# Gate and up tiles in pairs: wide products of both, then narrow ones, then the down product

## The chip, the cores and the metric

The kernel runs on one core of a Trainium2 chip. A core has a matrix engine (TensorE, "PE" in the profile, with its weight loads as "PEld"), VectorE ("DVE"), ScalarE ("ACT"), GpSimd ("POOL") and SyncE ("SP", which here starts nearly all transfers). Each engine works through its own queue in order. Matrix products are written to PSUM, which has eight banks of 128 x 512 float32; the other operands lie in SBUF.

The metric is the device time of one execution in microseconds (us), as a median of several.

## The reference: what is computed

Two decoder layers on x of 256 tokens by 1024 channels, in float32. Each layer is a feed-forward network (FFN), a mixer with three kinds of attention, and a second FFN:

```python
h = h + 0.5 * swiglu(rms_norm(h, ffn1_norm[l]), ffn1_w_gate[l], ffn1_w_up[l], ffn1_w_down[l])
h = h + hybrid_mixer(rms_norm(h, mix_norm[l]), w_in[l], ...)
h = h + 0.5 * swiglu(rms_norm(h, ffn2_norm[l]), ffn2_w_gate[l], ffn2_w_up[l], ffn2_w_down[l])

def swiglu(x, w_gate, w_up, w_down):
    return (jax.nn.silu(x @ w_gate) * (x @ w_up)) @ w_down
```

The gate and up matrices are 1024 x 2816, the down matrix 2816 x 1024. The change touches only the four FFNs.

## The kernel before

**Two-part numbers.** Every float32 operand of a large product is split into a high part (`wh`, `hh`, xhl's first half) and a low part, the rest (`wl`, `hl`, xhl's second half). A product is the sum high x high + high x low + low x high. For the normed input both parts lie side by side in the tile `xhl`, for each of eight k (128 channels each): 256 columns of high, 256 of low.

**Tiles of an FFN.** The hidden width of 2816 is cut into 22 tiles, f = 0 to 21, of 128. For a gate or up tile, `proj` takes one weight unit of 128 x 1024 and one PSUM bank of the kind `gu` (four banks). It issues eight matmuls 512 wide (the high weights with both parts of xhl, k = 0 to 7), and then eight that are 256 wide (the low weights with the high part). The bank then holds the main sum in its first half and the rest in its second. A down product `down(k)` multiplies one hidden tile with its weights: 24 matmuls of 256 columns into four banks of the kind `acc`. In the last FFN the down product has the tokens as its output rows, and takes 12 matmuls of 512.

**The loop.** For each f, `ffn` (line 356) emits: the gate tile; `gated`, which sums the bank's halves (ACT copies one half, L424; DVE adds the other, L425), multiplies by the norm's factor `norm.rb` (L430) and takes a tanh (L432); for f >= 4, the down product of hidden tile f - 4; `silu` (L450, L451); the up tile; and `hidden`, which sums the up bank (L424, L425), multiplies (L437) and splits the result into `hh` (L441) and `hl` (L444). The order in which these are emitted is the order on each engine's queue; it is written by hand (a manual schedule). A PSUM bank goes to the next tile of its kind when the last reader of the tile that had it is done; banks of one kind are handed out in the order in which they were released.

**Weights.** `Weights` keeps the list of weight units in the order of their use. A raw tile of 1 MB holds two units and is loaded by SP (line 90); five raw tiles can be in flight. `pump` splits one more unit: ACT writes the high part (`high`, L116), DVE the low part one unit later (`low`, L120). `pump` stops when seven units are split and not used; `take` hands out the next unit. The order of the list within an FFN is g(f), d(f - 4), u(f).

**Start and end of an FFN.** The norm's input arrives as `xhl`, k by k, from the tail of the stage before (`tail`, L317 on ACT for the high part, L320 on DVE for the low one), so that the last k, 6 and 7, come when the next FFN has begun. In FFN 1, 2 and 3 the first gate tile is therefore done in two groups of k, 0 to 5 and 6 to 7. The norm's factor comes out of two small products on PE: `norm.sums` (L340), then a power on DVE and POOL (L303, L304), then `norm.broadcast` (L347) and ACT's copy to `rb` (L349). They are placed inside the second and the third tile. Only with `rb` can `gated` finish, so four tiles (g0, u0, g1, u1) are done ahead, in the four `gu` banks. FFN 0 has a start of its own: g0 comes from the program's beginning, and a fifth tile, g2, goes to an `acc` bank. In FFN 3, `turn_trunk` (L383) transposes the residual on PE between u1 and g2. At the end, `tail` (or `finish` in FFN 3) does the last four down products, of f = 18 to 21, bank by bank.

## Time and profile before

| | us |
|---|---|
| median of 3 runs (lowest, highest) | 1060.74 (1060.62, 1060.92) |
| the profiled execution | 1060.79 |
| its span, from the first to the last instruction | 1059.0 |
| PE busy | 1049.5 (99%) |
| DVE busy | 829.4 (78%) |
| ACT busy | 594.9 (56%) |
| POOL busy | 163.7 (15%) |

Matmuls are pipelined: the duration of one in the profile is longer than its distance from the next. What a stream of matmuls costs is therefore read from the starts, not from the durations or the busy share. In rows of the timeline the first two numbers are start and duration in us; "x8" says that eight neighbours were merged; a bracket at the end tells how long the engine stood idle before and what released it. The mean granted clock of PE was 0.998 of full speed.

### The profile page before, as it was taken

The page shows a single profiled execution, that of the slowest core. Times are in us where ns is not written, and L with a number is a line of the kernel's source. Part 1 is how long each engine was busy: PE and PEld are TensorE (multiplying, and loading weights), DVE is VectorE, ACT ScalarE, POOL GpSimd, SP SyncE. Part 2 cuts the span into 40 slices and gives each one's busy share as a digit, 9 for nine tenths or more (in the row PEclk, how much of TensorE's full clock was granted, in tenths as well). Part 3 has the DMA queues.
Part 4 walks back from the last instruction along what each step waited for, and adds up shares of the span by engine and source line. Part 5 has one row for each costly group of instructions (what it writes and reads, how often), then busy time and mean ns, then how long its engine had stood idle before and what let it go on. Part 6 is the DMA issues. An engine that isn't in the chain of part 4 may idle for free.

```text
span 1059.0 us, 16914 instructions
## 1 busy us (share of the span) xinstructions
PE 1049.5 (99%) x6611; PEld 950.0 (90%) x6611; DVE 829.4 (78%) x1560; ACT 594.9 (56%) x1026; POOL 163.7 (15%) x184
## 2 busy tenths in 40 slices
PE   9999999999999999999999999999999999999998
PEld 8999999998799899999999999999978998888887
DVE  6998777779776897777789877777798779877774
ACT  6665554667654665555456555546766555645551
POOL 2004000267700100000010300003766000000000
PEclk9999999999999999999999999999999999999999
DMA  9576464465351365554645565555455214564531
GB/s 327 204 240 200 165 224 152 135 218 171 128 159 41 119 234 173 191 195 163 199 159 197 184 224 167 191 172 179 160 164 184 91 41 156 204 235 161 200 119 40
DMA packets 130912, 181.81 MB, mean 172 GB/s; under 512 B 7008, under 2 KB 104720, under 8 KB 130832
## 3 DMA queue, kind: packets, MB, share of 16 engines
q1 hardware_dynamic: 130512, 180.65, 50.7%
q8 instruction: 52, 0.85, 0.3%
q14 instruction: 28, 0.23, 0.1%
q10 hardware_dynamic: 320, 0.08, 0.0%
HBM read 179.67 MB, written 1.05 MB: 171 GB/s over the span
## 4 chain that ended last, share of the span: by engine, by line
PE 90%; DVE 5%; ACT 3%; issue 1%; DMA 1%; SPq 0%; ACTq 0%; DVEq 0%
PE ps_gu L293 59%; PE ps_acc L293 29%; DVE wl L120 2%; DVE score L728 1%; PE ps_gu L927 1%; DVE xhl L320 1%; DMA xin<-in_x_dram 1%; PE ps_gu L1027 0%; ACT wh L116 0%; ACT tmp L589 0%; DVE hres L352 0%; PE ps_gu L960 0%; ACT L710 0%; ACT L708 0%; DVE tmp L913 0%
## 5 line engine op out<-in xcount | busy, mean ns | idle before, releaser
L120 DVE TENSOR_TENSOR wl<-raw,wh 128x1024 fp32r<-128x1024 f32 (+2 forms) x343 | 416.8, 1221 | 21.8 <-ACT wh L116 21.5
L293 PE MATMUL ps_gu<-xhl,wh 128*128 128x512 f32 (+1 forms) x1408 | 352.6, 392 | 0.9 <-DVE xhl L320 0.7
L116 ACT CAST wh<-raw 128x1024 fp32r<-128x1024 f32 (+2 forms) x343 | 345.2, 1036 | 7.6 <-PE ps_gu L293 3.3
L293 PEld LDWEIGHTS ps_gu<-xhl,wh 128*128 128x128 f32 x1408 | 253.6, 189 | 47.6 <-DVE xhl L320 1.6
L293 PEld LDWEIGHTS ps_gu<-xhl,wl 128*128 128x128 f32 x1400 | 191.8, 190 | 13.7
L293 PE MATMUL ps_gu<-xhl,wl 128*128 128x256 f32 x1400 | 197.2, 283 | 0.0
L293 PE MATMUL ps_gu<-wh,xhl 128*128 128x512 f32 (+2 forms) x512 | 159.4, 381 | 0.0
L425 DVE TENSOR_TENSOR tmp<-ps_gu,tmp 128x256 f32<-128x256 f32 x175 | 74.1, 423 | 105.6 <-ACT tmp L424 105.5
L293 PE MATMUL ps_acc<-hl,wh 128*128 128x256 f32 x528 | 149.7, 284 | 0.0
L293 PE MATMUL ps_acc<-hh,wh 128*128 128x256 f32 x528 | 149.4, 283 | 0.0
L293 PE MATMUL ps_acc<-hh,wl 128*128 128x256 f32 x528 | 149.4, 283 | 0.0
L424 ACT COPY tmp<-ps_gu 128x256 f32<-128x256 f32 x175 | 64.7, 370 | 131.4 <-PE ps_gu L293 125.8
L293 PEld LDWEIGHTS ps_gu<-wh,xhl 128*128 128x128 f32 x512 | 95.7, 190 | 14.7
L293 PEld LDWEIGHTS ps_acc<-hl,wh 128*128 128x128 f32 x528 | 101.3, 192 | 0.3
L293 PEld LDWEIGHTS ps_acc<-hh,wl 128*128 128x128 f32 x528 | 101.4, 192 | 0.0
L293 PEld LDWEIGHTS ps_acc<-hh,wh 128*128 128x128 f32 x528 | 101.3, 192 | 0.0
L293 PE MATMUL ps_gu<-wl,xhl 128*128 128x512 f32 (+2 forms) x256 | 96.4, 377 | 0.0
L331 POOL TENSOR_TENSOR ssacc<-ssacc,tmp 128x512 f32<-128x512 f32 x10 | 13.0, 1297 | 512.5 <-ACT tmp L329 334.3
L432 ACT ACTIVATE tmp<-tmp 128x256 f32<-128x256 f32 x88 | 36.8, 418 | 85.1 <-DVE tmp L430 85.1
L441 ACT CAST hh<-tmp 128x256 fp32r<-128x256 f32 x80 | 32.6, 407 | 86.8 <-DVE tmp L437 86.8
L293 PEld LDWEIGHTS ps_gu<-wl,xhl 128*128 128x128 f32 x256 | 48.5, 190 | 6.8
L451 DVE TENSOR_TENSOR tmp<-tmp,rb 128x256 f32<-128x256 f32 x88 | 37.7, 429 | 3.0
(247 smaller groups left out, 1231.6 us busy)
## 6 DMA issues: line engine op xcount, KB each, us to landing
raw<-in_ffn_w_down_dram SPq DMA_DIRECT2D x44, 1024.0 KB, 6.7
raw<-in_ffn_w_gate_dram SPq DMA_DIRECT2D x43, 1024.0 KB, 7.2
raw<-in_ffn_w_up_dram SPq DMA_DIRECT2D x43, 1024.0 KB, 5.2
raw<-in_w_in_dram SPq DMA_DIRECT2D x24, 1024.0 KB, 5.1
raw<-in_w_out_dram SPq DMA_DIRECT2D x8, 1024.0 KB, 4.8
raw<-in_w_in_dram SPq DMA_DIRECT2D x4, 768.0 KB, 5.2
raw<-in_w_in_dram SPq DMA_DIRECT2D x4, 656.0 KB, 4.3
xin<-in_x_dram SPq DMA_DIRECT2D x4, 256.0 KB, 5.1
```

The lines of the kernel that those rows point to most:

```text
L116: self.nc.scalar.copy(hv, src)
L120: (engine or self.nc.vector).tensor_tensor(lv, self.srcs[self.n_low], hv.bitcast(F32), op=ALU.subtract)
L293: T.matmul(o, l, r, start=start, stop=stop, skip_group_check=True)
L320: V.scalar_tensor_tensor(self.l[:, m], hres[:, m] if src is None else src, gT[:, self.col + m:self.col + m + 1], self.h[:, m].bitcast(F32) ...
L331: G.tensor_tensor(self.acc, self.acc, sq, op=ALU.add)
L424: A.copy(o, ps[:, 1])
L425: V.tensor_tensor(o, ps[:, 0], o, op=ALU.add)
L432: A.activation(th, t_, AF.Tanh, scale=0.5)
L441: (V.tensor_copy if late else A.copy)(hh, t_)
L451: V.tensor_tensor(t_, t_, norm.rb, op=ALU.mult)
L728: V.scalar_tensor_tensor(sc, rl[:, i * n:(i + 1) * n], st["iw"][:, t, h:h + 1], st["cmask"][t] if first else sc, op0=ALU.mult, op1=ALU.add)
L927: T.transpose(b[:, j * P:(j + 1) * P], pj[i][:, j * P:(j + 1) * P], ident)
```

## The change

The list of weight units has u(f) before d(f - 4) now, and a new function `pair` takes two units and two banks at once. It issues all wide matmuls of both tiles, then all narrow ones of both; with groups of k, it does that group by group. The loop calls it for every f whose gate tile was not done early, so that the down product of f - 4 follows both tiles. At the start of FFN 1, 2 and 3, g0 and u0 are one pair in two groups of k; `norm.sums` follows behind it, and `norm.broadcast` stands between the wide and the narrow half of the second pair. In FFN 0 the start stays, and the tile u2 is now emitted ahead of `gated` for f = 2.

```diff
         for f in range(NF):
             half("g", f)
+            half("u", f)
             if f >= DOWN_LAG:
                 half("d", f - DOWN_LAG)
-            half("u", f)
...
+        def pair(groups=(range(KT),), between=None):
+
+            ws = [W.take() for _ in range(2)]
+            pss = [bank("gu").rearrange("p (a b) -> p a b", a=2) for _ in range(2)]
+            for ks in groups:
+                for w, ps in zip(ws, pss):
+                    for k in ks:
+                        mm(ps, w[0][:, k], norm.x[:, k], k == 0, False)
+                if between:
+                    between()
+                for w, ps in zip(ws, pss):
+                    for k in ks:
+                        mm(ps[:, 0], w[1][:, k], norm.h[:, k], False, k == KT - 1)
+            return pss
...
-            g0 = proj(groups=(range(6), range(6, KT)))
+            g0, u0 = pair((range(6), range(6, KT)))
+            norm.sums()
+            W.pump(3)
+            g1, u1 = pair(between=norm.broadcast)
             W.pump()
-            u0 = proj(norm.sums, 5)
-            W.pump(2)
-            g1 = proj(norm.broadcast, 7)
-            W.pump()
-            u1 = proj()
...
         for f in range(1, NF):
-            t_, th = gated(early[f] if f in early else proj())
+            g, u = (early[f], u1 if f == 1 else proj()) if f in early else pair()
+            t_, th = gated(g)
             if f >= DOWN_LAG:
                 down(f - DOWN_LAG)
                 W.pump()
             silu(t_, th)
-            hidden(f, t_, th, u1 if f == 1 else proj())
+            hidden(f, t_, th, u)
```

## The prediction

> **What bounds the kernel now.** I read the page first (one core, span, busy shares), then the chain of waits, then the timeline of TensorE (PE) inside one feed-forward layer (FFN), and last, around each start and end of an FFN, the rows of VectorE (DVE) beside those of PE.

> ```profile
> span 1059.0 us, 16914 instructions
> PE 1049.5 (99%) x6611; PEld 950.0 (90%) x6611; DVE 829.4 (78%) x1560; ACT 594.9 (56%) x1026; POOL 163.7 (15%) x184
> L120 DVE TENSOR_TENSOR wl<-raw,wh 128x1024 fp32r<-128x1024 f32 (+2 forms) x343 | 416.8, 1221 | 21.8 <-ACT wh L116 21.5
> ```

> PE is busy all the time, DVE three quarters of it, half of that with splitting weights (L120, 1.22 us each). So I sum PE's starts: the change pays where PE's stream gets shorter and costs where PE has to stop. Below, "FFN 0" and "FFN 1" are those of the first decoder layer, "FFN 2" and "FFN 3" those of the second. This is PE in an ordinary step (gate tile, up tile, down product) of FFN 0; columns: start, duration, then line, output and operands, form, count.

> ```profile
> 64.44 2.00 PE L293 MATMUL ps_gu<-xhl,wh 128*128 128x512 f32 x8
> 66.28 1.12 PE L293 MATMUL ps_gu<-xhl,wl 128*128 128x256 f32 x8
> 67.23 2.00 PE L293 MATMUL ps_gu<-xhl,wh 128*128 128x512 f32 x8
> 70.03 0.28 PE L293 MATMUL ps_acc<-hh,wh 128*128 128x256 f32 x1
> 72.91 2.00 PE L293 MATMUL ps_gu<-xhl,wh 128*128 128x512 f32 x8
> 198.02 5.47 PE ps_gu L293 x24
> ```

> From start to start, eight 512-wide matmuls after narrow ones take 66.28 - 64.44 = 1.84 us, eight 256-wide ones 0.95, a whole tile 2.79 to 2.80, a down product of 24 narrow ones 72.91 - 70.03 = 2.88 (0.120 each). The last row, from the chain of waits, is a run of 24 wide ones in the mixer: 5.47, against 3 x 1.84 = 5.52. Behind the first eight that is (5.47 - 1.84)/16 = 0.227 each, so a run pays 1.84 - 8 x 0.227 = 0.03 once, at its beginning; the entry into the narrow run gives 8 x 0.120 - 0.95 = 0.01 back.

> **The change, part by part.** *Fewer changes of width.* A pair is 16 wide and 16 narrow matmuls in 1.84 + 8 x 0.227 + 0.95 + 8 x 0.120 = 5.57 us, against 2 x 2.79 = 5.585. I take 0.02 us saved per pair (bounds: 0, and 0.03 if the narrow entry gave nothing). There are 19 pairs in FFN 0 (f = 3 to 21) and 22 in each other FFN, 85 in all. Ten of them (f = 3 and 4 of FFN 0, f = 0 to 3 of FFN 1 and 2) lie in stretches that I sum from their own rows below; the other 75 x 0.02 = **-1.5 us**. No matmul is removed.

> *The first pair in two k groups* (FFN 1, 2 and 3). FFN 1, PE and then DVE:

> ```profile
> 346.41 1.56 PE L293 MATMUL ps_gu<-xhl,wh 128*128 128x512 f32 x6
> 349.05 0.90 PE L293 MATMUL ps_gu<-xhl,wh 128*128 128x512 f32 x2 [0.37 <-DVE xhl L320]
> 350.03 2.00 PE L293 MATMUL ps_gu<-xhl,wh 128*128 128x512 f32 x8
> 356.05 0.60 PE L293 MATMUL ps_acc<-cst,y_n 128*128 128x128 f32 x4
> 356.41 2.09 PE L293 MATMUL ps_gu<-xhl,wh 128*128 128x512 f32 x8
> 359.29 2.00 PE L293 MATMUL ps_gu<-xhl,wh 128*128 128x512 f32 x8
> ...
> 348.25 1.14 DVE L320 SCALAR_TENSOR_TENSOR xhl<-hres,gT,xhl 128x256 fp32r<-128x256 f32 x2 [0.25 <-ACT xhl L317]
> 358.32 0.42 DVE L425 TENSOR_TENSOR tmp<-ps_gu,tmp 128x256 f32<-128x256 f32 x1 [0.73 <-ACT tmp L424]
> 361.05 0.42 DVE L425 TENSOR_TENSOR tmp<-ps_gu,tmp 128x256 f32<-128x256 f32 x1
> ```

> The gate tile took 350.03 - 346.41 = 3.62 us instead of 2.79, since k = 6 and 7 of xhl came late: 0.83 lost. With gate and up of k = 0 to 5 first, PE has 2 x (6 x 0.23 + 6 x 0.12) = 4.2 us to do before it wants k = 6, at 350.6, and DVE has them at 348.25 + 1.14 = 349.4. So 0.83 comes back in FFN 1, and the same in FFN 3 (row below); in FFN 2 nothing waits there now.

> *Sums and broadcast.* Both small products stay, one behind the first pair, one between the wide and the narrow half of the second. The broadcast takes 356.41 - 356.05 = 0.36, and the run behind it is 2.09 - 2.00 = 0.09 longer; I take 0.37 and 0.09 for the sums too. So: first pair 5.58, sums 0.37, 16 wide 5.47 - 8 x 0.227 + 0.09 = 3.74, broadcast 0.36, 16 narrow 1.91 + 0.09 = 2.00. In FFN 1 the broadcast starts at 346.41 + 5.58 + 0.37 + 3.74 = 356.10 (was 356.05), and f = 2 is reached at 358.46 (was 359.29).

> *What becomes late: the PSUM banks.* `gu` has four banks, so pair f writes the banks of pair f - 2, and can't before DVE's add (L425) has read them. A whole pair wants both banks within 1.84 us; before, the up tile came 2.79 after the gate tile, or 5.7 with the down product between. In FFN 1 the adds of f = 0 hang on the broadcast and shift with it by 0.05: gate read at 358.32 + 0.05 + 0.42 = 358.79, up at 361.05 + 0.47 = 361.52. Release to start takes 0.06, and the eight wide matmuls after such a stop 1.97 (both from the next fence). So g2 starts at 358.85, 0.39 late; u2 could start at 360.82 and starts at 361.58; the wide half ends at 363.55, the narrow (1.91) at 365.46. f = 3, whose banks are read by then, ends at 371.03. Before, f = 4 started at 359.29 + 4 x 2.795 = 370.47. FFN 1 reaches f = 4 **0.56 late**, its gain of 0.83 included.

> FFN 2 has the same chain without the gain, and FFN 3 has transposes (L383) before f = 2:

> ```profile
> 534.53 1.55 PE L293 MATMUL ps_gu<-xhl,wh 128*128 128x512 f32 x6
> 543.88 2.09 PE L293 MATMUL ps_gu<-xhl,wh 128*128 128x512 f32 x8
> 546.77 2.00 PE L293 MATMUL ps_gu<-xhl,wh 128*128 128x512 f32 x8
> ...
> 545.79 0.42 DVE L425 TENSOR_TENSOR tmp<-ps_gu,tmp 128x256 f32<-128x256 f32 x1 [0.72 <-ACT tmp L424]
> 548.53 0.41 DVE L425 TENSOR_TENSOR tmp<-ps_gu,tmp 128x256 f32<-128x256 f32 x1
> ...
> 869.03 1.56 PE L293 MATMUL ps_gu<-xhl,wh 128*128 128x512 f32 x6
> 872.64 2.00 PE L293 MATMUL ps_gu<-xhl,wh 128*128 128x512 f32 x8
> 881.93 1.91 PE L383 MATMUL ps_acc<-cst,hres 128*128 128x128 f32 x16
> ```

> FFN 2: f = 2 is reached at 534.53 + 12.05 = 546.58; the broadcast ends at 544.58 instead of 543.88, so the adds shift by 0.70: g2 at 546.97, u2 at 549.70, f = 4 at 559.15 against 546.77 + 11.18 = 557.95: **1.20 late**. FFN 3: 872.64 - 869.03 = 3.61 shows the same 0.83; the 16 transposes (1.9 us) keep PE busy while the banks are read: **-0.83**.

> FFN 0 keeps its own start: g2 goes to an `acc` bank, and the pairs begin at f = 3.

> ```profile
> 24.87 2.14 PE L293 MATMUL ps_gu<-xhl,wh 128*128 128x512 f32 x8 [0.17 <-DVE tmp L425]
> 26.84 1.10 PE L293 MATMUL ps_gu<-xhl,wl 128*128 128x256 f32 x8
> 27.78 2.00 PE L293 MATMUL ps_gu<-xhl,wh 128*128 128x512 f32 x8
> 41.83 2.00 PE L293 MATMUL ps_gu<-xhl,wh 128*128 128x512 f32 x8
> ...
> 24.39 0.42 DVE L425 TENSOR_TENSOR tmp<-ps_gu,tmp 128x256 f32<-128x256 f32 x1
> 29.69 0.42 DVE L425 TENSOR_TENSOR tmp<-ps_gu,tmp 128x256 f32<-128x256 f32 x1 [0.22 <-ACT tmp L424]
> 37.72 0.42 DVE L425 TENSOR_TENSOR tmp<-ps_gu,tmp 128x256 f32<-128x256 f32 x1
> ```

> Here a bank wait stands already: u2 starts at 24.87, 0.06 after the add of g0 ended (24.81), and its wide run takes 26.84 - 24.87 = 1.97. The order of release gives u3 the bank of g1 (read at 29.69 + 0.42) and u4 the bank of u2 (read at 37.72 + 0.42 = 38.14; DVE first reads g0 at 24.39, with five tiles done on PE, and takes 29.69 - 24.39 = 5.3 us per f). After: g3 at 27.78 as now; u3 wanted at 29.62, free at 30.17; pair done 34.05; u4 wanted at 35.89, free at 38.20: **2.3 us of stop**. Today the down product stands in between and hides it. Behind u4 on PE stand the narrow half and down product 0; ACT's copy of g4 waits for that half, but DVE, at f = 3 until about 45, does not miss it. Pair 4 is done at 42.08, the down product at 44.96, where f = 5 began at 41.83: **3.13 late**. From f = 5 on each pair has a down product behind it and two steps' time for its banks.

> *Down products behind the pair, at the end of an FFN* (0, 1, 2). The last hidden tile hangs on the gate tile's end and on DVE:

> ```profile
> 179.56 1.12 PE L293 MATMUL ps_gu<-xhl,wl 128*128 128x256 f32 x8
> 181.12 0.43 DVE L425 TENSOR_TENSOR tmp<-ps_gu,tmp 128x256 f32<-128x256 f32 x1
> 185.02 0.43 DVE L451 TENSOR_TENSOR tmp<-tmp,rb 128x256 f32<-128x256 f32 x1
> 186.79 0.42 DVE L425 TENSOR_TENSOR tmp<-ps_gu,tmp 128x256 f32<-128x256 f32 x1 [1.35 <-ACT tmp L424]
> 188.04 0.43 DVE L444 TENSOR_TENSOR hl<-tmp,hh 128x256 fp32r<-128x256 f32 x1
> ```

> The last gate tile ends at 179.56 + 0.95 = 180.51. From there DVE needs 0.61 to its add, 4.33 to the end of L451, then, with no wait for the up tile, the 1.68 from L425 to the end of L444: hl stands 6.62 after the gate's end. PE wants it after the up half 0.96, the down product 2.88, 18 products 2.16 and one more 0.12: 6.12. I take 0.45 us per FFN net of the small stop that is there now (bounds 0 and 0.7): **+1.35**.

> *Order of loads and splits.* Down halves now load and split behind up halves, in SP's queue as in ACT's and DVE's. Each raw tile is still one of three per two steps, and seven halves are split ahead; after a pair took two, five are left, 1.5 steps. I take 0; with that cover gone a tile waits for a split, 1.22 us (L120) at each place.

> **Sum:** -1.5 (widths) + 3.13 + 0.56 + 1.20 - 0.83 (starts) + 1.35 (ends) = +3.9. The profiled execution took 1060.79, 1.79 more than its span and 0.05 above the median of 1060.74: 1060.8 + 3.9 = **1064.7**.

> **Rivals.** *The banks don't bind* (the other side). If the pool hands out banks in another order, or DVE is earlier with f = 2, the stops go: f = 5 of FFN 0 begins at 27.78 + 2 x 5.57 + 2.88 = 41.80 instead of 44.96, f = 4 of FFN 1 and 2 1.44 earlier each (358.46 + 2 x 5.57 = 369.60); 1064.7 - 6.0 = 1058.7, faster. It decides at u4's bank: free before 35.9 instead of 38.1. Against it: the wait at 24.87 shows the first released bank given out first, and DVE's adds of f = 2 have no idle time to give.

> *Half stops*: u4 doesn't wait, the others do: 1064.7 - 2.4 = 1062.3.

> *The clock.* After an idle stretch of 1.74 us in the mixer the granted clock fell to a half for 3.4 us:

> ```profile
> 267.19 0.88 PE L293 MATMUL ps_acc<-va,pT 128*128 128x65 f32 x6 [1.74 <-ACT pT L929]
> 268.47:271.88 3.41, 3.41 (x10) 2.63 (x8) 3.24 (x13) 2.14 (x4) 3.33 (x3) 0.50 0.72 209
> ```

> Ten matmuls where 15 would run: 1.7 us. The stop before u4 is 2.3 us by starts, 2.15 by records, longer than that one. If it brings the same, 1064.7 + 1.7 = 1066.4. [...]

> *Wide runs gain nothing by merging*: the change doesn't do what its order is for, 85 x 0.02 = 1.7 more, 1066.4; the row of 24 speaks against it.

> **How the numbers follow.** Forecast 0.45; clock 0.25; banks don't bind 0.12; half stops 0.12; no gain from merging 0.06. The range takes in half stops with ends that cost nothing (1062.3 - 1.35, about 1060.9) and the clock with ends at their upper bound (1066.4 + 0.75, about 1067.2): 1060.9 to 1067.2, which leaves out the bank rival. 0.2% is 2.1 us, about what a measurement of this kernel can tell: faster means below 1058.6, slower above 1062.9. The bank rival lies on the lower line and gives its chance to both sides; half stops lie below the upper one, mostly "same": faster 0.08, same 0.17, slower 0.75.

> **What would show it.** PE in an ordinary step: 16 wide, 16 narrow, 24 down in 8.45 us instead of 8.47. In FFN 0 a wait of about 2 us of a wide `ps_gu` matmul for DVE's L425 near 38 us, with f = 5 near 45. In FFN 1 and 2 two stops of 0.4 and 0.75 at f = 2, none in FFN 3. No wait for xhl L320 at a start. A stop of half a microsecond at the last hidden tile of FFN 0, 1 and 2. A clock below full right behind 38 us makes the clock rival true. The prediction is wrong if PE passes f = 4 of FFN 0 without a stop, or if it begins to wait for wl or raw tiles in ordinary steps.

## The result, and the profile after

| | before | after |
|---|---|---|
| median of 6 runs, side by side, us | 1060.62 | 1064.6 |
| lowest and highest | 1059.06, 1060.92 | 1063.07, 1067.75 |
| the profiled execution | 1060.79 | 1064.65 |
| its span | 1059.0 | 1062.9 |
| granted clock in it | 0.998 | 0.998 |

The ratio is 1.0046 with an interval of 1.0031 to 1.0062: slower, by 4 us. Another four runs of the same kernel gave 1062.85 to 1067.73 (below). PE still sets the time (busy 1049.3 us, 99% of the span), and the view of the waits puts its new idle time in one row. Columns: engine, tile and line, what it waited for, us in total, times, the longest. The add that was L425 is L440 now.

```profile
PE ps_gu L293 <- DVE tmp L440: 4.6, 7, 2.2
```

Before, the same row had 0.2 us, one time. The ordinary step, and FFN 0 where that wait is longest, are these rows of PE's timeline. (Here and below, the last row of a stretch can show fewer matmuls than the run has, as x5 does, because the window that was read ends there.)

```profile
27.70 2.00 PE L293 MATMUL ps_gu<-xhl,wh 128*128 128x512 f32 x8
30.09 2.12 PE L293 MATMUL ps_gu<-xhl,wh 128*128 128x512 f32 x8 [0.39 <-DVE tmp L440]
...
33.95 2.00 PE L293 MATMUL ps_gu<-xhl,wh 128*128 128x512 f32 x8
38.10 3.50 PE L293 MATMUL ps_gu<-xhl,wh 128*128 128x512 f32 x8 [2.15 <-DVE tmp L440]
...
46.42 3.82 PE L293 MATMUL ps_gu<-xhl,wh 128*128 128x512 f32 x16
...
51.98 0.28 PE L293 MATMUL ps_acc<-hh,wh 128*128 128x256 f32 x1
...
54.87 1.32 PE L293 MATMUL ps_gu<-xhl,wh 128*128 128x512 f32 x5
```

Step f = 5 takes 54.87 - 46.42 = 8.45 us; it took 8.47. Its 32 matmuls of a pair take 51.98 - 46.42 = 5.56. In FFN 0, u3 and u4 stop for DVE's add, as the brackets at 30.09 and 38.10 say (0.39 and 2.15 us of idle records; 0.55 and 2.31 from start to start, over the usual 0.227), and f = 5 comes 46.42 - 27.70 = 18.72 us after g3, where it was 41.83 - 27.78 = 14.05. The reason is in DVE's timeline, the add of u2, which stands where it stood before (37.72):

```profile
37.63 0.41 DVE L440 TENSOR_TENSOR tmp<-ps_gu,tmp 128x256 f32<-128x256 f32 x1
```

The starts of FFN 1, 2 and 3 in PE's timeline:

```profile
349.48 2.94 PE L293 MATMUL ps_gu<-xhl,wh 128*128 128x512 f32 x12
...
353.69 1.09 PE L293 MATMUL ps_gu<-xhl,wh 128*128 128x512 f32 x4
...
355.09 0.56 PE L293 MATMUL ps_acc<-ones,ssacc 128*128 128x1 f32 x4
...
362.11 2.09 PE L293 MATMUL ps_gu<-xhl,wh 128*128 128x512 f32 x8 [0.32 <-DVE tmp L440]
364.83 2.08 PE L293 MATMUL ps_gu<-xhl,wh 128*128 128x512 f32 x8 [0.63 <-DVE tmp L440]
...
374.23 1.09 PE L293 MATMUL ps_gu<-xhl,wh 128*128 128x512 f32 x4
...
538.34 2.91 PE L293 MATMUL ps_gu<-xhl,wh 128*128 128x512 f32 x12
...
543.92 0.50 PE L293 MATMUL ps_acc<-ones,ssacc 128*128 128x1 f32 x4
...
550.84 2.06 PE L293 MATMUL ps_gu<-xhl,wh 128*128 128x512 f32 x8 [0.32 <-DVE tmp L440]
553.56 2.09 PE L293 MATMUL ps_gu<-xhl,wh 128*128 128x512 f32 x8 [0.66 <-DVE tmp L440]
...
562.96 3.36 PE L293 MATMUL ps_gu<-xhl,wh 128*128 128x512 f32 x14
...
874.08 2.94 PE L293 MATMUL ps_gu<-xhl,wh 128*128 128x512 f32 x12
...
886.23 1.91 PE L383 MATMUL ps_acc<-cst,hres 128*128 128x128 f32 x16
```

The wait for xhl (L320) is gone: k = 0 to 5 of both tiles are 12 wide matmuls in one row, and the last four follow at 353.69 with no bracket. FFN 1 and FFN 2 stop twice each at f = 2, FFN 3 not at all. From the start to f = 4 FFN 1 takes 374.23 - 349.48 = 24.75, FFN 2 562.96 - 538.34 = 24.62, and FFN 3 886.23 - 874.08 = 12.15 to its transposes.

The end of FFN 0, the last hidden tile's products:

```profile
192.47 0.28 PE L293 MATMUL ps_acc<-hh,wl 128*128 128x256 f32 x1
192.78 0.35 PE L293 MATMUL ps_acc<-hh,wh 128*128 128x256 f32 x1
193.15 0.39 PE L293 MATMUL ps_acc<-hl,wh 128*128 128x256 f32 x1
193.38 0.28 PE L293 MATMUL ps_acc<-hh,wl 128*128 128x256 f32 x1
```

Three steps take 193.38 - 192.47 = 0.91 instead of 3 x 0.120: 0.55 lost, where 0.15 was lost before; PE waits for the two parts of the hidden tile, which DVE writes just then (the high part at L456 from 192.34 on, the low part at L459, L444 before, from 192.67 on).

Last, the clock. Windows of the profile of after (columns: the stretch and its us, then busy us and count of PE, PEld, DVE, ACT and POOL, the granted clock, DMA share, GB/s):

```profile
35.06:38.47 3.41, 1.26 (x6) 0.70 (x6) 3.31 (x8) 1.62 (x3) 0.00 (x0) 1.00 0.00 0
38.47:41.88 3.41, 3.41 (x11) 2.76 (x10) 3.16 (x6) 2.33 (x5) 0.00 (x0) 0.50 0.29 54
270.58:273.99 3.41, 2.12 (x14) 1.94 (x15) 3.38 (x12) 2.71 (x6) 2.00 (x1) 1.00 0.00 0
```

Right behind u4's stop PE ran at half clock for 3.41 us. The mixer, which had its half clock in the profile of before (268.47:271.88), has none in this one: the third row is the window with its idle stretch, and none at half clock follows before PE's work ends. So both profiled executions contain one such stretch, at different places, and their difference, 3.9 us, is free of it.

### The profile page after: what moved, and what is told of

The parts are those of the page before. It is cut to its first block, busy times and chain, and to the rows that moved or that the text cites. A ratio compares the mean times of both kernels' runs of the same rounds, so it can differ in the third digit from the quotient of the medians.

```text
span 1062.9 us, 16911 instructions
## 1 busy us (share of the span) xinstructions
PE 1049.3 (99%) x6611; PEld 950.0 (89%) x6611; DVE 823.5 (77%) x1560; ACT 588.6 (55%) x1026; POOL 161.7 (15%) x184
## 3 DMA queue, kind: packets, MB, share of 16 engines
HBM read 179.67 MB, written 1.05 MB: 170 GB/s over the span
## 4 chain that ended last, share of the span: by engine, by line
PE 89%; DVE 6%; ACT 3%; issue 1%; DMA 1%; SPq 0%; ACTq 0%; DVEq 0%
PE ps_gu L293 58%; PE ps_acc L293 30%; DVE wl L120 2%; DVE score L742 1%; ACT wh L116 1%; PE ps_gu L941 1%; DMA xin<-in_x_dram 1%; PE ps_gu L1041 0%; DVE tmp L440 0%; ACT tmp L603 0%; PE ps_gu L974 0%; ACT L724 0%; ACT L722 0%; DVE tmp L927 0%; DVE bkT L650 0%
## 5 line engine op out<-in xcount | busy, mean ns | idle before, releaser
L120 DVE TENSOR_TENSOR wl<-raw,wh 128x1024 fp32r<-128x1024 f32 (+2 forms) x343 | 416.3, 1220 | 22.1 <-ACT wh L116 21.9
L116 ACT CAST wh<-raw 128x1024 fp32r<-128x1024 f32 (+2 forms) x343 | 345.2, 1036 | 7.7 <-PE ps_gu L293 3.3
L293 PE MATMUL ps_gu<-xhl,wh 128*128 128x512 f32 (+1 forms) x1408 | 338.6, 391 | 4.6 <-DVE tmp L440 4.6
L293 PEld LDWEIGHTS ps_gu<-xhl,wh 128*128 128x128 f32 x1408 | 259.2, 189 | 57.2 <-DVE tmp L440 3.7
L293 PEld LDWEIGHTS ps_gu<-xhl,wl 128*128 128x128 f32 x1400 | 180.6, 191 | 7.1
L293 PE MATMUL ps_gu<-xhl,wl 128*128 128x256 f32 x1400 | 183.8, 283 | 0.0
L440 DVE TENSOR_TENSOR tmp<-ps_gu,tmp 128x256 f32<-128x256 f32 x175 | 73.5, 420 | 115.5 <-ACT tmp L439 115.5
L293 PE MATMUL ps_gu<-wh,xhl 128*128 128x512 f32 (+2 forms) x512 | 158.4, 379 | 0.0
L293 PE MATMUL ps_acc<-hl,wh 128*128 128x256 f32 x528 | 149.7, 284 | 0.0
L293 PE MATMUL ps_acc<-hh,wh 128*128 128x256 f32 x528 | 149.6, 283 | 0.1
L293 PE MATMUL ps_acc<-hh,wl 128*128 128x256 f32 x528 | 149.4, 283 | 0.0
L293 PEld LDWEIGHTS ps_gu<-wh,xhl 128*128 128x128 f32 x512 | 94.8, 188 | 14.5
L456 ACT CAST hh<-tmp 128x256 fp32r<-128x256 f32 x80 | 32.6, 407 | 125.4 <-DVE tmp L452 125.4
L293 PEld LDWEIGHTS ps_acc<-hl,wh 128*128 128x128 f32 x528 | 101.4, 192 | 0.6 <-DVE hl L459 0.6
L293 PEld LDWEIGHTS ps_acc<-hh,wh 128*128 128x128 f32 x528 | 101.3, 192 | 0.6 <-issue 0.6
L293 PEld LDWEIGHTS ps_acc<-hh,wl 128*128 128x128 f32 x528 | 101.4, 192 | 0.0
L293 PE MATMUL ps_gu<-wl,xhl 128*128 128x512 f32 (+2 forms) x256 | 95.8, 374 | 0.0
L293 PEld LDWEIGHTS ps_gu<-wl,xhl 128*128 128x128 f32 x256 | 48.2, 188 | 6.6
```

Source lines behind the costliest of these rows:

```text
L116: self.nc.scalar.copy(hv, src)
L120: (engine or self.nc.vector).tensor_tensor(lv, self.srcs[self.n_low], hv.bitcast(F32), op=ALU.subtract)
L293: T.matmul(o, l, r, start=start, stop=stop, skip_group_check=True)
L440: V.tensor_tensor(o, ps[:, 0], o, op=ALU.add)
L456: (V.tensor_copy if late else A.copy)(hh, t_)
```

## The experiments

Before was run 25 times beside the first four kernels (median 1060.52) and 29 times beside the other four (1060.28). Since half-clock stretches come and go from run to run, as the last section tells, I also compare runs with the same mean granted clock: before takes 1059.1 at 1.000, 1060.65 at 0.998 and 1062.1 at 0.996.

**Is it u2's bank?** Only the tile u2 of FFN 0 goes to an `acc` bank, so that u3 and u4 find `gu` banks that were read long before. The four `acc` banks of the down products are then taken at f = 4.

```diff
-        acc = [bank("acc") for _ in range(4)]
         for f in range(1, NF):
-            g, u = (early[f], u1 if f == 1 else proj()) if f in early else pair()
+            g, u = (early[f], u1 if f == 1 else proj(tag="acc")) if f in early else pair()
...
+            if f == DOWN_LAG:
+                acc = [bank("acc") for _ in range(4)]
```

> The changed kernel, but the tile u2 of FFN 0 goes to an acc bank (acc banks are idle until the first down product, whose four banks are now taken at f = 4), so that u3 and u4 get banks read long before. My theory, that the stops at f = 3 and 4 are waits for PSUM banks: both stops go (0.55 and 2.3 us), u2's own wait at 24.8 too, and f = 5 of FFN 0 begins near 41.3 us instead of 46.4; no half clock behind it. The time falls by 3.6 us, and by 1.5 more where the half clock went with the stop. The rival, that u4 is late because its split weights are late in the new order of units: u4 stops as before, f = 5 stays between 45 and 46.4, no change in time.

Measured: 1061.54, ratio 1.001 (1.0 to 1.0019). PE's timeline of this kernel:

```profile
27.79 3.82 PE L293 MATMUL ps_gu<-xhl,wh 128*128 128x512 f32 x16
...
33.35 3.82 PE L293 MATMUL ps_gu<-xhl,wh 128*128 128x512 f32 x16
...
41.80 4.25 PE L293 MATMUL ps_gu<-xhl,wh 128*128 128x512 f32 x16
```

Both stops are gone, pairs 3 and 4 run as 16 wide matmuls without a bracket, and f = 5 comes 41.80 - 27.79 = 14.01 after g3. A smaller wait has moved on: the 16 wide of f = 5 take 4.25 instead of 3.82, because u5 now finds its bank 0.4 late. The order of the weight units is the same as in the change, so late weights are not the cause of the stops. At clock 0.998 the kernel takes 1061.65 against 1064.54 for the change, 2.9 less and not 3.6. By PE's starts the stops give back 17.16 - 14.01 = 3.15 (17.16 is the change at full clock, below), and u2's own wait 0.43 (from g2 to g3 5.60 instead of 6.03); of that, 0.43 is lost again at f = 5 and 0.19 at f = 9, which takes 8.75 instead of 8.56.

**The same for f = 2 of FFN 1 and 2.** On top of that, the pair of f = 2 goes to `acc` banks where a mixer or an FFN follows.

```diff
-        def pair(groups=(range(KT),), between=None):
+        def pair(groups=(range(KT),), between=None, tag="gu"):
-            pss = [bank("gu").rearrange("p (a b) -> p a b", a=2) for _ in range(2)]
+            pss = [bank(tag).rearrange("p (a b) -> p a b", a=2) for _ in range(2)]
...
-            g, u = (early[f], u1 if f == 1 else proj(tag="acc")) if f in early else pair()
+            g, u = (early[f], u1 if f == 1 else proj(tag="acc")) if f in early else pair(tag="acc" if f == 2 and nxt else "gu")
```

> As the run with u2 in an acc bank, and both tiles of f = 2 in acc banks in FFN 1 and 2 too. Theory: the two stops at f = 2 of FFN 1 and 2 go as well; from the start of the first pair to the start of f = 4 it takes 23.2 us instead of 24.75 in each. 6.6 us below the changed kernel without half clocks, about 1056.4 to 1058, 0.25% below the kernel before. Rival (weights late, or DVE's chain itself bounds these steps): PE stops at the same places for DVE or ACT, and less than 2 us is won in FFN 1 and 2 together.

Measured: 1058.58, ratio 0.9983 (0.9973 to 0.9994), faster than before. PE's timeline, FFN 1:

```profile
346.43 2.92 PE L293 MATMUL ps_gu<-xhl,wh 128*128 128x512 f32 x12
...
358.54 3.82 PE L293 MATMUL ps_acc<-xhl,wh 128*128 128x512 f32 x16
...
369.67 2.68 PE L293 MATMUL ps_gu<-xhl,wh 128*128 128x512 f32 x11
```

f = 2 writes `ps_acc` at 358.54 without a wait, and f = 4 is reached after 369.67 - 346.43 = 23.24 us instead of 24.75; FFN 2 takes 23.16 instead of 24.62. The row for DVE's add is gone from the view of the waits, though the 16 wide of f = 5 in FFN 0 still take 4.24. At clock 0.998 the kernel takes 1058.76, 5.8 below the change, where 6.6 was expected. Other banks for five tiles turn the change from 4 us slower to 2 us faster, so the banks are the cause of the loss and not the order of the products as such.

**The last step in the old order.** f = 21 alone goes back to gate, down product, up.

```diff
-            half("u", f)
+            if f < NF - 1:
+                half("u", f)
             if f >= DOWN_LAG:
                 half("d", f - DOWN_LAG)
+            if f == NF - 1:
+                half("u", f)
```

In the loop, g is then a single `proj()` at that f, and u a `proj()` behind the down product.

> The changed kernel, but the last step (f = 21) in the old order: gate tile, down product, up tile. Theory: DVE gets the last gate tile one wide run earlier against the end, the stop at the last hidden tile in FFN 0, 1 and 2 falls from about 0.55 to 0.15 us, 1.2 us less in all, everything ahead unchanged. Rival: the stop hangs on the up tile's end, not on the gate tile's, and stays at about 0.5.

Measured: 1064.32 in the median of four runs (1063.44 to 1065.33), ratio 1.0043 (1.0028 to 1.0058): by the median not to be told from the change. By the profiles it is: span 1061.7 against 1062.9, both with one half-clock stretch. PE's timeline:

```profile
27.56 2.00 PE L296 MATMUL ps_gu<-xhl,wh 128*128 128x512 f32 x8
...
37.98 2.11 PE L296 MATMUL ps_gu<-xhl,wh 128*128 128x512 f32 x8 [2.15 <-DVE tmp L443]
...
44.72 3.59 PE L296 MATMUL ps_gu<-xhl,wh 128*128 128x512 f32 x15
...
190.92 0.28 PE L296 MATMUL ps_acc<-hh,wh 128*128 128x256 f32 x1
191.09 0.39 PE L296 MATMUL ps_acc<-hl,wh 128*128 128x256 f32 x1
191.31 0.28 PE L296 MATMUL ps_acc<-hh,wl 128*128 128x256 f32 x1
```

The last hidden tile loses 191.31 - 190.92 - 2 x 0.12 = 0.15 again, as before the change; FFN 1 and 2 each take 20.01 us from the start of f = 21 to their last down product, where the change takes 20.40 and 20.39. Three times 0.39 back is the 1.2 between the spans. This profile gives something else too: u4 has its stop of 2.15 us at 37.98, but no half clock behind it, and f = 5 comes 44.72 - 27.56 = 17.16 after g3, not 18.72. The half clock in the profile of after was worth the difference, 1.56.

**The order without the merging.** The down product goes behind both tiles, but each tile is done on its own, and the starts are the old ones.

```diff
-            g, u = (early[f], u1 if f == 1 else proj()) if f in early else pair()
+            g, u = (early[f], u1 if f == 1 else proj()) if f in early else (proj(), proj())
```

> Order alone: units in the order gate, up, down and the down product behind both tiles, but each tile wide and then narrow by itself, and the start of each FFN as in the kernel before. Theory: an ordinary step takes 8.47 us as before (the merged one 8.45), the start of FFN 1 to 3 is as before, with the wait for xhl. In FFN 0 u4 still comes too early: wanted at 36.2, its bank free near 38.2, f = 5 begins at 44.0 instead of 41.8, 2.2 us late (1.5 more with a half clock); no stop at f = 2 of FFN 1 and 2; the small stop at the last hidden tile goes (0.15 in each of three). Sum +1.75 us against the kernel before, 1062.4. Rival, that merging the wide runs is what brings the bank stops: f = 5 of FFN 0 begins at 41.8 and the time is that of before.

Measured: 1061.57, ratio 1.0021 (1.0008 to 1.0035); at full clock 1060.69 against 1059.1, 1.6 more. PE's timeline:

```profile
38.04 2.12 PE L293 MATMUL ps_gu<-xhl,wh 128*128 128x512 f32 x8 [1.88 <-DVE tmp L440]
...
43.83 1.55 PE L293 MATMUL ps_gu<-xhl,wh 128*128 128x512 f32 x6
```

u4 still stops, for 1.88 us; u3 doesn't, nor does f = 2 of FFN 1 and 2, since a gate tile's narrow half stands again between the two banks. An ordinary step takes 8.47 us as before (f = 5 begins at 43.83, f = 6 at 52.30). So the long stop belongs to the down product's move, and the short ones to the merging. Two of the ten runs took 1065.4 at a clock of 0.997, more than their clock accounts for; that stays open.

**The new start alone.** Before, with the first pair in two groups of k, `norm.sums` behind it, and from g1 on the old code.

```diff
-            g0 = proj(groups=(range(6), range(6, KT)))
-            W.pump()
-            u0 = proj(norm.sums, 5)
-            W.pump(2)
+            g0, u0 = pair((range(6), range(6, KT)))
+            norm.sums()
+            W.pump(3)
             g1 = proj(norm.broadcast, 7)
             W.pump()
             u1 = proj()
```

> The kernel before, with the first pair alone: g0 and u0 of FFN 1, 2 and 3 as a pair in two groups of k, the sums behind it, then g1 (broadcast inside), u1 and the old loop. Theory: the wait for k = 6 and 7 of xhl goes, 0.83 us in FFN 1 and in FFN 3, 0.1 in FFN 2; the broadcast comes 0.8 earlier, so DVE's adds of f = 0 do too, and no bank stop appears at f = 2: 1.8 us below the kernel before. Rival, that the first pair itself brings the bank stops: PE waits for DVE's add at f = 2 and 1 us or less is won.

Measured: 1058.95, ratio 0.9991 (0.9982 to 1.0); at clock 0.998 1058.88 against 1060.65, 1.8 less. PE's timeline, FFN 1:

```profile
344.76 2.94 PE L293 MATMUL ps_gu<-xhl,wh 128*128 128x512 f32 x12
...
356.91 2.00 PE L293 MATMUL ps_gu<-xhl,wh 128*128 128x512 f32 x8
```

f = 2 is reached after 12.15 us instead of 359.29 - 346.41 = 12.88, with no stop there: this part of the change pays by itself.

**Pairs in the middle alone.** Before, with pairs only for f = 7 to 20, in all four FFNs; every other step and the starts as before.

```diff
+    def single(fi, f):
+        return f < 7 or f == NF - 1
...
-            t_, th = gated(early[f] if f in early else proj())
+            if f not in early and single(fi, f):
+                g, u = proj(), None
+            else:
+                g, u = (early[f], u1 if f == 1 else proj()) if f in early else pair()
+            t_, th = gated(g)
...
-            hidden(f, t_, th, u1 if f == 1 else proj())
+            hidden(f, t_, th, u or proj())
```

The list of units has u before d for the same steps.

> The kernel before, with pairs only at f = 7 to 20 of each FFN; the start, the steps to f = 6 and the last one are as before. 56 pairs of 0.02 us: 1.1 us below the kernel before, no stop anywhere. Rival, that a merged run saves nothing: no change. Rival, that the down product behind the pair makes DVE late in ordinary steps: slower than before.

Measured: 1058.7, ratio 0.9989 (0.998 to 0.9998); at full clock 1058.04 against 1059.09, 1.05 less for 56 pairs, 0.019 us each. Nothing waits for a split weight or a raw tile that didn't before.

**The three together.** The banks of the second experiment, the last step of FFN 0, 1 and 2 in the old order, and step f = 5 of FFN 0 in the old order, because u5 waited there.

```diff
+    def single(fi, f):
+        return (fi < 3 and f == NF - 1) or (fi == 0 and f == 5)
```

> The changed kernel with both repairs: the tiles of f = 2 in acc banks in FFN 0, 1 and 2, the last step of these three in the old order, and f = 5 of FFN 0 in the old order too (in the run with acc banks u5 still waited 0.4 us there). Theory: no wait of PE for a bank in any FFN, 1.6 us below the run with acc banks: 1055.7 with a full clock throughout, 3.4 us or 0.3% below the kernel before. Rival, that the stops move on to the next steps: PE waits for L440 at f = 6 or later and the time stays near 1057.

Measured: 1058.92 in 12 runs, ratio 0.9982 (0.9974 to 0.9991): faster than both kernels, though by its median not faster than the second experiment. At full clock it takes 1056.2 against 1059.09 (2.9 less), at 0.998 1057.55 against 1060.65 (3.1 less); seven of its twelve runs had a clock of 0.997 or 0.996, which gives half of that back.

The expectation was not met in full: against the second experiment the kernel gains 1.1 us at full clock (1057.3 there) and 1.2 at 0.998, not 1.6. That is what the last steps are worth; the old order at f = 5 gained nothing. From f = 5 to f = 21 FFN 0 takes 136.20 us in both kernels, because the wait moved on to the up tile of f = 9, as the rival said that it would. PE's timeline:

```profile
77.59 2.11 PE L299 MATMUL ps_gu<-xhl,wh 128*128 128x512 f32 x8 [0.32 <-DVE tmp L446]
```

**The changed kernel again.** No edit.

> The changed kernel once more, beside the others on one chip, for the clock behind the stop of u4. If a stop of 2.1 us (by records) brings a half clock as the idle stretches of 1.7 in the mixer do, more of its executions than of those of the other kernels show a clock below 0.998, and a full clock is rare; if not, the share with a full clock is that of the kernel before, about one in three. At a full clock it stands 4.0 us above the kernel before.

Measured: 1066.01, 1067.73, 1067.55 and 1062.85, median 1066.78; ratio 1.0055 (1.0037 to 1.0072). With the first six, the ten runs have a median of 1065.3. Three of the four have a clock below 0.998, where the kernel before has one of 29 beside them; the one at full clock stands 3.8 above 1059.09. The windows of its profile show a half clock behind u4's stop again, and a second one in the mixer:

```profile
35.70:39.11 3.41, 1.25 (x6) 1.01 (x6) 3.34 (x6) 2.37 (x5) 0.00 (x0) 1.00 0.02 5
39.11:42.52 3.41, 3.41 (x15) 3.03 (x14) 3.12 (x7) 2.40 (x5) 0.00 (x0) 0.50 0.52 148
793.46:796.87 3.41, 1.69 (x13) 1.41 (x12) 3.38 (x9) 2.79 (x5) 0.55 (x1) 1.00 0.25 103
796.87:800.28 3.41, 3.41 (x12) 2.83 (x12) 3.38 (x14) 2.33 (x5) 3.33 (x3) 0.50 0.54 161
```

## Why the prediction was right

Forecast 1064.7, measured 1064.6 in the first six runs and 1065.3 in all ten. The terms, each from PE's starts:

| step of the prediction | predicted | measured |
|---|---|---|
| fewer changes of width, 75 pairs | -1.5 | -1.5 (0.02 per step; 1.05 for 56 pairs alone) |
| FFN 0, stops of u3 and u4 | +3.13 | 17.16 - 14.05 = +3.1 at full clock; 18.72 - 14.05 = +4.7 with the half clock |
| FFN 1, start and stops | +0.56 | 24.75 - 24.06 = +0.69 |
| FFN 2 | +1.20 | 24.62 - 23.42 = +1.20 |
| FFN 3 | -0.83 | 12.15 - 12.90 = -0.75 |
| ends of FFN 0, 1 and 2 | +1.35 | 3 x 0.39 = +1.2 |
| sum | +3.9 | +3.9, half clock aside |

- **Widths.** Right, and shown by the pairs in the middle alone; the order without the merging keeps its step of 8.47, so the gain is the merging's. The rival that merging gains nothing falls.
- **Starts.** The wait for xhl went as predicted. FFN 1 and FFN 3 fall short by 0.13 and 0.08. About 0.06 of that in FFN 1 is a cause that I left out: the sums now come so early that they seem to wait for their input `ssacc` (the four take 0.56 at 355.09, and 0.50 in FFN 2 at 543.92). The rest isn't accounted for.
- **Banks.** Both the places and the sizes are right. The rival in which the banks don't bind was priced 6.0 lower, at 1058.7; made true by the second experiment, it took 1058.58. What made it false in the changed kernel is what the prediction named, the order of release and DVE's add of u2 at 37.63.
- **Ends.** Right within 0.06 per FFN, and undone by the third experiment.
- **Loads and splits.** Taken at nothing, and nothing waited.
- **The clock.** Here the prediction was right by luck. It gave 0.25 to the half clock behind u4's stop, as a fourth part of the cases that shifts the whole time by 1.7. In two of three profiles of kernels with this stop it is there, at 1.56. The median did not move by it in the first six runs, because the base of 1060.74 already held one half-clock stretch, in the mixer, and the typical run of the changed kernel had one as well. In all ten runs it shows: half of them took 1066.0 or more, and the later four have their median at 1066.78, where the clock rival stood (1066.4). By these few profiles the chance was too low, and its effect is a step in some runs, not a shift of all.

## What to carry to other kernels

Before a product is moved out from between two tiles, ask what it was covering: here the down product hid 2.15 us in which a PSUM bank waited for a DVE that was two steps behind (at u2 when PE came to u4), and the same reordering paid as soon as those tiles got banks that nobody had to empty first. Where the matrix engine is 99% busy, sum the starts of its rows by place: gains of 0.02 us in 75 places and losses of 0.4 to 3 us in six were each readable from the trace of before. Stops of the matrix engine of 1.72 to 2.15 us were followed by 3.41 us at half clock in some profiles here and not in others, and behind u4's stop that cost 1.56 us: compare runs at the same granted clock before judging a microsecond.

## What was not expected of the hardware

```profile
265.06:268.47 3.41, 1.67 (x13) 1.44 (x13) 3.38 (x10) 2.41 (x5) 1.16 (x1) 1.00 0.06 24
...
787.30:790.71 3.41, 2.37 (x13) 1.84 (x11) 3.16 (x8) 2.80 (x7) 0.00 (x0) 1.00 0.68 274
790.71:794.12 3.41, 2.73 (x17) 2.42 (x18) 3.38 (x14) 2.75 (x7) 2.61 (x1) 1.00 0.15 31
```

```profile
33.69:37.10 3.41, 2.15 (x11) 1.47 (x9) 3.15 (x6) 2.40 (x5) 0.00 (x0) 1.00 0.05 18
37.10:40.51 3.41, 2.53 (x13) 2.19 (x14) 3.12 (x7) 1.91 (x5) 0.00 (x0) 1.00 0.02 5
...
791.45:794.86 3.41, 1.69 (x14) 1.46 (x13) 3.38 (x10) 2.42 (x5) 1.15 (x1) 1.00 0.08 32
```

In the first, the window before the half clock has 1.67 us of PE in 3.41; the mixer's second idle stretch is as long (1.72 us), but falls on two windows, 2.37 and 2.73 busy, and no half clock follows. In the second, u4's stop of 2.15 us falls on two windows (2.15 and 2.53 busy) and is not followed by one, while the mixer's, with 1.69, is. In the profile of after the stop lies in one window with 1.26 busy, in its second set in one with 1.25. Over the seven profiles that show such a stretch, so that the windows can be laid, all nine windows with 1.25 to 1.69 us of PE were followed by a half clock, and none with 1.91 or more; nothing lay between 1.69 and 1.91. In these profiles, then, both the length of a stop and its place in the windows went with a half clock. The windows in which PE's work ends are left out of this count, and they don't all fit it: one of 0.46 us in the profile of after and one of 0.70 in that of the kernel with f = 2 in `acc` banks were followed by a half clock, but one of 1.55, in the kernel with the three parts together, was not. So PE's busy time as the profile records it doesn't account for every case.

**The time comes in steps of about 1.55 us** (before: 1059.1 at a clock of 1.000, 1060.65 at 0.998, 1062.1 at 0.996). Ahead of the end of PE's work, the profiles at 0.998 hold one half-clock stretch each, those at 0.997 and 0.996 (the three parts together, the changed kernel again) two, and those at 1.000 (the order alone, the pairs in the middle) none in the first 890 us, which were read. Before has two idle stretches in the mixers, of 1.74 us ending at 267.19 and here:

```profile
791.39 0.88 PE L293 MATMUL ps_acc<-va,pT 128*128 128x65 f32 x6 [1.72 <-ACT pT L929]
```

They are 524.20 us apart, 153.57 windows, and in its profile a half clock follows the first alone. Of the 54 runs beside the experiments 22 had a clock of 1.000, 29 of 0.998 and 3 of 0.996. In the kernel with the three parts together the two are nearer to a whole number:

```profile
266.73 1.14 PE L299 MATMUL ps_acc<-va,pT 128*128 128x65 f32 x6 [1.74 <-ACT pT L953]
...
789.19 1.34 PE L299 MATMUL ps_acc<-va,pT 128*128 128x65 f32 x6 [1.72 <-ACT pT L953]
```

522.46 us is 153.07 windows, and in its profile a half clock follows both. By their clocks, seven of its runs had about two stretches, four had one, one had none. That the distance in windows sets how many stretches a run has, and that the median of that kernel suffers from this alone, is my estimate from these two profiles, worked out after the fact; no kernel was run to move an idle stretch on purpose, and it is not shown.

For the change there was an extra stretch in a part of the runs. The fourteen runs of the kernels with the 2.15 us stop (the change twice, and the one with its last step in the old order) had 22 by their clocks (three runs at 0.995, counted as three stretches each, four at 0.996 as two, five at 0.998 as one, two at 1.000 as none), 1.6 a run against 35 in 54, 0.65 a run, before. At 1.55 us each that is an estimated 1.4 us on the mean beside the 3.9 at equal clock (1063.0 against 1059.1 with none, 1064.5 against 1060.65 with one).
